# One kernel, one change: GpSimd copies the parts of the mixer's input with even and odd tokens side by side, and two attention groups load from the copies

## The chip, the cores and the metric

The kernel runs on one core of a Trainium2 chip. Its time is the device time of one execution in microseconds (us), as the median of several executions. The profile shows one further execution, instruction by instruction, for TensorE (PE, with its weight loads PEld), VectorE (DVE), ScalarE (ACT), GpSimd (POOL) and SyncE (SP, which issues DMAs).

## The reference, cut to what matters

The kernel computes two layers of a decoder trunk on 256 tokens of width 1024, all in float32. Each layer is a half-step of SwiGLU, a mixer, and another half-step of SwiGLU. The mixer normalises its input and multiplies it with one wide matrix; the columns feed three branches, of which the dilated attention is the one concerned:

```python
A_CONFIGS = ((128, 1), (512, 4), (2048, 16))      # (window, dilation) of the three head groups

def dilated_group(q, k, v, window, dilation):
    # gather each residue class mod dilation by stride, then banded attention inside each class
    ...

def hybrid_mixer(h, cos, sin, w_in, ...):
    a_qkv, b_q, b_kv, c_q, c_k, c_v, c_glow, c_r, gate_pre = jnp.split(h @ w_in, splits, axis=-1)
    a_q = apply_rope(rmsnorm(a_qkv[:, :, 0], a_q_norm), cos, sin)
    a_k = apply_rope(rmsnorm(a_qkv[:, :, 1], a_k_norm), cos, sin)
    y_a = dilated_mixer(a_q, a_k, a_qkv[:, :, 2])
    ...
    return merged @ w_out
```

## The kernel before, in words

**Precision and weights.** A float32 product is made of three fast passes (high x high, high x low, low x high), so every weight is split into a high part `hi` and a rest `lo`. `emit_dma` (L168) loads blocks of weights of up to 1 MB into a `raw` buffer. `emit_split` (L179) makes of each block one or two units: ACT casts `hi` (L191) and DVE subtracts to get `lo` (L192). A unit is 128 x 1024 numbers in nearly all cases. There are NRAW = 4 raw buffers and NHL = 5 pairs of `hi` and `lo`; `LD` and `LS` say how far ahead of their use the loads and splits are written. Every weight of the kernel goes through these buffers.

**The mixer's input.** `norm_parts` (L281) makes for each of the eight feature tiles one buffer `hl` of 128 features x 512: the high parts of the 256 tokens, then the low parts. The buffers named `a` in the profile come from one pool of NA.

**Projections.** `tok_proj` (L537) multiplies 512 columns of weights for two sets of 128 tokens. The tokens are what TensorE loads as its stationary 128 x 128 operand, the weights (512 columns) stream through it. For each feature tile k and each set there are three matmuls, L545 to L547. The two results lie in two PSUM banks `p`. The first head group takes tokens 0 to 127 and 128 to 255; the other two groups take the even tokens and the odd tokens (sets 2 and 3), and `tokens` (L306) reads them from `hl` with a step of two. Each of these two groups has three projections (q, k, v) in each of two layers, with 8 feature tiles x 2 sets x 3 = 48 matmuls each: 576 matmuls with a step of two in all.

**After a projection.** `rope` (L557) rotates the result. Of the mean square, DVE makes one number per token and head, and GpSimd raises it to the power -0.5 (`rsqrt`, L255, recorded as L256). For k, DVE takes that result (L601), multiplies the rotated rows with it (L603), and TensorE transposes them (`turned`, L583), before the scores can be computed.

**What sets the order.** The program is recorded by a tile framework whose scheduler fixes the order on each engine beforehand, from the data each instruction needs, the buffers that are free, and its own estimate of durations. On the chip each engine follows its list in order; an instruction whose data are not there holds up all behind it on that engine.

Of the kernel before, what the change touches and what calls it, by code (L numbers as in the profile page):

```python
# [11 lines left out]
F32R = mybir.dt.float32r  # L12
# [5 lines left out]
P = 128  # L18
T = 256
NT = T // P  # L20
# [51 lines left out]
def trunk_kernel(ctx, tc, x, positions, norm_ffn1, w_ffn1_in, w_ffn1_out, norm_mix, w_in, a_q_norm, a_k_norm,  # L72
                 b_q_norm, b_k_norm, b_sinks, c_gate_up, c_gate_bias, c_out_norm, w_branch, w_out,
                 norm_ffn2, w_ffn2_in, w_ffn2_out, const, out):
    nc = tc.nc
# [4 lines left out]
    sm = ctx.enter_context(tc.tile_pool(name="sm", bufs=1))  # L80
    pp = ctx.enter_context(tc.tile_pool(name="pp", bufs=1, space=PSUM))

    NA, NW, NRAW, NHL = 32, 12, 4, 5
    LD, LS = 4, 4
    uid = [0]

    def nm(s):
        uid[0] += 1
        return f"{s}{uid[0]}"

    def big(dt=F32):
        b = ap_.tile([P, 512], dt, tag="a", bufs=NA, name=nm("a"))
        return b
# [9 lines left out]
    def bank(tag):  # L103
        b = pp.tile([P, 512], F32, tag=tag, bufs=BANKS[tag], name=nm("p"))
        return b

    def f(a):
        return a.bitcast(F32)
# [21 lines left out]
    for l in range(DEPTH):  # L130
        for half in range(2):
# [8 lines left out]
            if l == DEPTH - 1 and half == 1:  # L140
                for e in range(2):
                    for k in range(0, KF, 4):
                        n = min(4, KF - k)
# [56 lines left out]
    def chunk():  # L200
        u = cur[0]
        cur[0] += 1
        ahead(u)
        return splits.pop(u)
# [69 lines left out]
    def begin_norm(which, l):  # L274
        n = Normed()
        n.col = which * 16 + l * 8
        n.hl, n.h, n.l = [], [], []
        n.acc, n.ssq = None, None
        return n

# [25 lines left out]
    def tokens(a, tt):  # L306

        return a[:, tt * P:(tt + 1) * P] if tt < NT else a[:, tt - NT:T:2]
# [46 lines left out]
    def joined(dst, ps):  # L355
        low = sm.tile([P, T], F32, tag="low", bufs=3, name=nm("low"))
        nc.scalar.copy(low, ps[:, T:2 * T])  # L357
        nc.vector.tensor_add(dst, ps[:, 0:T], low)  # L358

    n0 = begin_norm(0, 0)  # L360
    n0.src = []
    for mp in range(KD // 2):
# [153 lines left out]
    def mixer(l, n, nxt):  # L516
# [13 lines left out]
        def fill():  # L530
            for name in list(streams):
                owed[name] = owed.get(name, 0.0) + RATES[name]
                while owed[name] >= 1.0:
                    owed[name] -= 1.0
                    step(name)

        def tok_proj(cols, per, first=False, sets=(0, 1)):  # L537
            ps = [bank("mm") for _ in range(NT)]
            for k0 in range(0, KD, per):
                wh, wl = chunk()  # L540
                for k in range(k0, k0 + per):
                    for t in range(NT):
                        xh, xl = tokens(n.h[k], sets[t]), tokens(n.l[k], sets[t])
                        o = ps[t][:, 0:cols]
                        nc.tensor.matmul(o, xh, wh[:, k - k0, :], start=(k == 0), stop=False)  # L545
                        nc.tensor.matmul(o, xh, wl[:, k - k0, :], start=False, stop=False)  # L546
                        nc.tensor.matmul(o, xl, wh[:, k - k0, :], start=False, stop=(k == KD - 1))  # L547
                if not first:
                    fill()
            return ps  # L550
# [418 lines left out]


        psb = tok_proj(272, 4, True)
        next(fin)
        ps = bank("mm")
# [24 lines left out]
        for g in range(3):  # L998
            sets = (0, 1) if g == 0 else (2, 3)
            qs, sc = q_rope(tok_proj(512, 2, sets=sets), tabs[0], sets)  # L1000
            ks = k_rope(tok_proj(512, 2, sets=sets), tabs[1], 8, sets)
            v = v_side(tok_proj(512, 2, sets=sets), 0, 512, sets)
            ready.append(attend(qs, sc, ks, v, (C_MASK, C_MASK + 512, C_MASK + 640)[g], g == 0, lambda h: h // 2,
                                lambda h: h, None, group_stats(g), group_done(g)))
# [34 lines left out]
        for mp in range(KD // 2):  # L1039
# [13 lines left out]
            h, lo = big(F32R), big(F32R)  # L1053
# [15 lines left out]
    for l in range(DEPTH):  # L1069
        nmix = begin_norm(1, l)  # L1070
        swiglu(cur_n, lambda m: norm_tile(nmix, m), [lambda: late_loads(n0), lambda: None, late_gains, rope_tables] if l == 0 else (),
               first=keep_x if l == 0 else None)
        nf2 = begin_norm(2, l)
        mixer(l, nmix, lambda m: norm_tile(nf2, m))
        if l + 1 < DEPTH:
            cur_n = begin_norm(0, l + 1)
            swiglu(nf2, lambda m: norm_tile(cur_n, m))
        else:
            xo = [[None] * 2 for t in range(NT)]

            def token_major(t, e):
                def go():
                    ps = bank("at")
                    for i in range(4):
                        nc.tensor.transpose(ps[:, i * P:(i + 1) * P], xT[4 * e + i][:, t * P:(t + 1) * P], ident)
                    xo[t][e] = big()
                    nc.scalar.copy(xo[t][e], ps)
                return go

            swiglu(nf2, None, [lambda: None] * 2 + [token_major(t, e) for t in range(NT) for e in range(2)], True)  # L1090
# [25 lines left out]
```

## Time and profile before

| | |
|---|---|
| median of 3 runs | 1451.25 us (1451.22 to 1451.53) |
| profiled execution's own time | 1451.08 us |
| its span, first to last instruction | 1449.3 us |
| PE busy | 1436.9 us (99%) |
| DVE, ACT, POOL busy | 1047.5 us (72%), 840.5 us (58%), 135.1 us (9%) |
| mean share of the 16 DMA engines | 51.3% for the weights' queue |

The profile gives for each group of instructions their source line, the tiles they write and read (`p<-hi,a` writes a PSUM bank from a weight part and an input part), their number and mean duration, and what ended the idle time before them. Matmuls overlap: one of 512 columns is recorded with some 0.39 us, but the next starts earlier, so the cost of one is read from the distance of their starts. Some matmuls of plain float32 appear twice in the profile for one in the program.

### The profile page before, as it was taken

Reading aid. Unit: us, or ns where it says so; the run is one execution under the profiler, and the core shown is the slowest. Engines: PE = TensorE matmul, PEld = TensorE weight load, DVE = VectorE, ACT = ScalarE, POOL = GpSimd, SP = SyncE. Lnnn points to the kernel's source line nnn. Section 1 sums busy time; section 2 is a strip of 40 time slices with the busy share of each in tenths; the row PEclk is TensorE's granted clock in tenths of the full one; section 3 lists DMA queues with packets and bytes.
Section 4 is the critical chain, followed back from the end, with each engine's and each line's share of the span. In section 5 each row is a group of like instructions: output and inputs, shape, how many; then the busy total and the mean of one; then the engine's idle time right before and its main releaser. Section 6 shows DMA issues by size and latency. Waiting matters only on the chain.

```text
span 1449.3 us, 23359 instructions
## 1 busy us (share of the span) xinstructions
PE 1436.9 (99%) x9114; PEld 1268.9 (88%) x9114; DVE 1047.5 (72%) x1923; ACT 840.5 (58%) x1432; POOL 135.1 (9%) x124
## 2 busy tenths in 40 slices
PE   7999999999999999999999999999999999999998
PEld 6888898888899998888888888988878999988887
DVE  6787667888677686776677766688876767776753
ACT  6666456556747456665556655466477464566642
POOL 2030002223111000000000000032210200000000
PEclk9999999999999999999999999999999999999999
DMA  9655564443452565555556555643444426565551
GB/s 298 206 179 185 175 211 154 146 145 117 151 170 74 169 221 178 182 196 180 195 177 201 178 186 164 210 156 130 147 145 146 146 74 218 175 191 188 180 202 53
DMA packets 214702, 246.31 MB, mean 170 GB/s; under 512 B 6524, under 2 KB 183376, under 8 KB 214592
## 3 DMA queue, kind: packets, MB, share of 16 engines
q1 hardware_dynamic: 214016, 243.48, 51.3%
q0 software_dynamic: 544, 1.33, 0.4%
q8 instruction: 71, 1.16, 0.3%
q14 instruction: 39, 0.32, 0.1%
q10 hardware_dynamic: 32, 0.01, 0.0%
HBM read 243.76 MB, written 1.05 MB: 169 GB/s over the span
## 4 chain that ended last, share of the span: by engine, by line
PE 94%; DVE 2%; ACT 1%; POOL 1%; DMA 1%; issue 1%; SPq 0%; DVEq 0%
PE p L350 30%; PE p L353 16%; PE p L333 6%; PE p L331 6%; PE p L332 6%; PE p L545 6%; PE p L547 5%; PE p L546 5%; PE p L654 2%; PE p L690 2%; PE p L583 1%; PE p L491 1%; PE p L490 1%; PE p L492 1%; PE p L699 1%; PE p L878 1%
## 5 line engine op out<-in xcount | busy, mean ns | idle before, releaser
L191 ACT CAST hi<-raw 128x1024 fp32r<-128x1024 f32 (+3 forms) x468 | 483.1, 1036 | 475.8 <-PE p L350 234.1
L192 DVE TENSOR_TENSOR lo<-raw,hi 128x1024 fp32r<-128x1024 f32 (+3 forms) x468 | 561.6, 1206 | 241.6 <-PE p L353 141.1
L350 PE MATMUL p<-a,hi 128*128 128x512 f32 x1936 | 467.8, 393 | 2.9 <-ACT hi L191 1.5
L350 PEld LDWEIGHTS p<-a,hi 128*128 128x128 f32 x1936 | 355.5, 189 | 73.4 <-ACT hi L191 2.3
L353 PEld LDWEIGHTS p<-a,lo 128*128 128x128 f32 x1936 | 249.7, 191 | 10.3
L353 PE MATMUL p<-a,lo 128*128 128x256 f32 x1936 | 253.2, 283 | 0.0
L333 PE MATMUL p<-a,lo 128*128 128x256 f32 x768 | 219.1, 286 | 0.0
L331 PE MATMUL p<-a,hi 128*128 128x256 f32 x768 | 218.3, 286 | 0.0
L332 PE MATMUL p<-a,hi 128*128 128x256 f32 x768 | 218.1, 284 | 0.0
L256 POOL TENSOR_TENSOR s<-s,neghalf 128x8 f32<-128x8 f32 (+2 forms) x42 | 87.6, 2086 | 977.5 <-DVE s L316 656.9
L545 PE MATMUL p<-hi,a 128*128 128x512 f32 (+1 forms) x416 | 163.7, 394 | 0.0
L546 PE MATMUL p<-lo,a 128*128 128x512 f32 (+1 forms) x416 | 162.3, 390 | 0.0
L547 PE MATMUL p<-hi,a 128*128 128x512 f32 (+1 forms) x416 | 160.9, 389 | 0.0
L333 PEld LDWEIGHTS p<-a,lo 128*128 128x128 f32 x768 | 147.1, 192 | 1.4 <-issue 1.4
L332 PEld LDWEIGHTS p<-a,hi 128*128 128x128 f32 x768 | 147.2, 192 | 0.7 <-issue 0.3
L331 PEld LDWEIGHTS p<-a,hi 128*128 128x128 f32 x768 | 146.7, 192 | 1.1 <-issue 0.7
L545 PEld LDWEIGHTS p<-hi,a 128*128 128x128 f32 x416 | 79.3, 191 | 15.9 <-issue 0.7
L547 PEld LDWEIGHTS p<-hi,a 128*128 128x128 f32 x416 | 79.1, 191 | 15.0 <-issue 0.3
L546 PEld LDWEIGHTS p<-lo,a 128*128 128x128 f32 x416 | 79.4, 191 | 14.5 <-issue 0.3
L357 ACT COPY low<-p 128x256 f32<-128x256 f32 x200 | 73.7, 372 | 25.9 <-PE p L353 23.1
L358 DVE TENSOR_TENSOR w<-p,low 128x256 f32<-128x256 f32 x176 | 72.3, 416 | 0.0
L675 ACT ACTIVATE w<-w,st,s 128x128 f32<-128x128 f32 (+1 forms) x96 | 47.8, 503 | 11.7 <-DVE st L669 11.7
(224 smaller groups left out, 1290.5 us busy)
## 6 DMA issues: line engine op xcount, KB each, us to landing
raw<-in_w_ffn_in_dram SPq DMA_DIRECT2D x87, 1024.0 KB, 5.1
raw<-in_w_in_dram SPq DMA_DIRECT2D x76, 1024.0 KB, 5.0
raw<-in_w_ffn_out_dram SPq DMA_DIRECT2D x34, 1024.0 KB, 5.2
raw<-in_w_branch_dram SPq DMA_DIRECT2D x24, 512.0 KB, 3.4
raw<-in_w_ffn_out_dram SPq DMA_DIRECT2D x12, 768.0 KB, 4.5
raw<-in_w_out_dram SPq DMA_DIRECT2D x8, 1024.0 KB, 5.9
raw<-in_w_in_dram SPq DMA_DIRECT2D x4, 512.0 KB, 3.5
a<-in_x_dram SPq DMA_DIRECT2D x4, 256.0 KB, 5.1
```

The costliest lines, as they stand in the source:

```text
L191: nc.scalar.copy(hi[:, k:k + cut], r[:, k:k + cut])
L192: nc.vector.tensor_sub(lo[:, k:k + cut], r[:, k:k + cut], f(hi[:, k:k + cut]))
L256: nc.gpsimd.tensor_tensor(dst, src, neghalf[:, 0:n], op=OP.pow)
L331: nc.tensor.matmul(ps, wh, xh, start=first, stop=False)
L332: nc.tensor.matmul(ps, wh, xl, start=False, stop=False)
L333: nc.tensor.matmul(ps, wl, xh, start=False, stop=last)
L350: nc.tensor.matmul(ps, w[0][:, k, :], xhl[k], start=first and k == 0, stop=False)
L353: nc.tensor.matmul(ps[:, 0:T], w[1][:, k, :], xhl[k][:, 0:T], start=False, stop=last and k == nk - 1)
L357: nc.scalar.copy(low, ps[:, T:2 * T])
L545: nc.tensor.matmul(o, xh, wh[:, k - k0, :], start=(k == 0), stop=False)
L546: nc.tensor.matmul(o, xh, wl[:, k - k0, :], start=False, stop=False)
L547: nc.tensor.matmul(o, xl, wh[:, k - k0, :], start=False, stop=(k == KD - 1))
```

## The change

`tok_proj` no longer reads the even and odd tokens with a step. When the first projection with sets 2 and 3 comes to feature tile k, GpSimd copies `hl` of that tile into a new buffer `eo`, with the even tokens first and the odd ones behind them (both for the high and for the low parts), and all six projections of the layer's two groups load from the copies. That is 8 copies of 128 x 512 in a layer, 16 in all. To make room, the `a` pool grows by 8 buffers, and there is one raw buffer less and one pair of `hi` and `lo` less; loads and splits are written one step less ahead.

```diff
-    NA, NW, NRAW, NHL = 32, 12, 4, 5
-    LD, LS = 4, 4
+    NA, NW, NRAW, NHL = 40, 12, 3, 4
+    LD, LS = 3, 3
...
-        n.hl, n.h, n.l = [], [], []
+        n.hl, n.h, n.l, n.eo = [], [], [], []
...
-                        xh, xl = tokens(n.h[k], sets[t]), tokens(n.l[k], sets[t])
+                        if sets[t] < NT:
+                            xh, xl = tokens(n.h[k], sets[t]), tokens(n.l[k], sets[t])
+                        else:
+                            if len(n.eo) == k:
+                                n.eo.append(big(F32R))
+                                nc.gpsimd.tensor_copy(n.eo[k].rearrange("p (h o i) -> p h o i", h=2, o=2),
+                                                      f(n.hl[k]).rearrange("p (h i o) -> p h o i", h=2, o=2))
+                            xh, xl = (n.eo[k][:, h * T + (sets[t] - NT) * P:h * T + (sets[t] - NT + 1) * P] for h in range(2))
```

All later lines move down by seven: L545 to L547 become L552 to L554, L583 becomes L590, L603 becomes L610, L907 becomes L914.

The scheduler makes a new order of this. On TensorE in the first layer, where the first group's v projection (banks p310, p311) ends and the second group's q projection (p321, p322) begins, the order before is:

```order
L547 MATMUL p311_2623<-hi85_2572,a219_2098 128x512
L545 MATMUL p321_2716<-hi86_2626,a184_1650 128x512
...
L547 MATMUL p321_2716<-hi87_2653,a199_1806 128x512
L907 MATMUL p317_2703<-pair_88,w316_2651 128x2 x4
L583 MATMUL p323_2736<-cst_70,a277_2472 128x128 x4
L583 MATMUL p325_2743<-cst_70,a284_2488 128x128 x4
...
L546 MATMUL p321_2716<-lo88_2672,a205_1940 128x512
L583 MATMUL p327_2766<-cst_70,a297_2590 128x128 x4
L547 MATMUL p321_2716<-hi88_2671,a205_1940 128x512
```

Here a184 to a219 are the eight input parts `hl`, a277 and a284 the first group's rotated q, a297 its rotated k of tokens 0 to 127, and w316 a product for the gated linear attention. The same place with the change:

```order
L554 MATMUL p311_2617<-hi85_2618,a219_2092 128x512
L914 MATMUL p317_2697<-pair_88,w316_2643 128x2 x4
L590 MATMUL p325_2732<-cst_70,a277_2466 128x128 x4
L590 MATMUL p327_2739<-cst_70,a284_2482 128x128 x4
L590 MATMUL p331_2768<-cst_70,a297_2584 128x128 x4
L552 MATMUL p321_2710<-hi86_2647,a323_2716 128x512
...
L554 MATMUL p322_2711<-hi87_2663,a330_2760 128x512
L552 MATMUL p367_2922<-hi90_2748,a323_2716 128x512
```

The product of w316 and all three transposes, that of a297 among them, now stand ahead of the whole strided q projection, of which 26 matmuls stood before the transpose of a297 until now; behind its first four feature tiles (copies a323 to a330) comes the beginning of the next projection (p367).

On GpSimd at the same place, before; s301 and s308 are the powers for the first group's k of tokens 0 to 127 and 128 to 255:

```order
L256 TENSOR_TENSOR s288_2498<-s287_2496,neghalf_96 128x8
L256 TENSOR_TENSOR s301_2600<-s300_2598,neghalf_96 128x8
L256 TENSOR_TENSOR s308_2617<-s307_2615,neghalf_96 128x8
L256 TENSOR_TENSOR s350_2892<-s349_2890,neghalf_96 128x8
L256 TENSOR_TENSOR s357_2908<-s356_2906,neghalf_96 128x8
```

And with the change:

```order
L256 TENSOR_TENSOR s288_2492<-s287_2490,neghalf_96 128x8
L256 TENSOR_TENSOR s301_2594<-s300_2592,neghalf_96 128x8
L548 CAST a323_2716<-a184_1644 128x512
L548 CAST a324_2724<-a188_1655 128x512
L548 CAST a329_2752<-a195_1788 128x512
L548 CAST a330_2760<-a199_1800 128x512
L256 TENSOR_TENSOR s308_2611<-s307_2609,neghalf_96 128x8
L548 CAST a335_2786<-a205_1934 128x512
L548 CAST a336_2794<-a209_1946 128x512
L548 CAST a346_2857<-a215_2080 128x512
L548 CAST a347_2865<-a219_2092 128x512
```

All eight copies stand behind the power s301, four of them ahead of s308. In the second layer both engines show the same pattern.

## Rows read from the trace of the kernel before

**Rows 1.** The profile's page: busy us, share of the span, number of instructions.
```profile
PE 1436.9 (99%) x9114; PEld 1268.9 (88%) x9114; DVE 1047.5 (72%) x1923; ACT 840.5 (58%) x1432; POOL 135.1 (9%) x124
```

**Rows 2.** Waits of PE: line, releaser, us in total, times, longest.
```profile
PE p L260 <- DMA cst<-in_const_dram: 2.9, 1, 2.9
...
PE p L583 <- DVE a L603: 0.6, 2, 0.3
```

**Rows 3.** Two stretches of PE: length, PE busy (instructions), PEclk, DMA share, GB/s.
```profile
243.06:253.94 10.88, 10.88 (x50) 1.00 0.30 98
253.94:258.84 4.90, 4.90 (x22) 1.00 0.65 214
```

**Rows 4.** POOL's copies of 128 x 512: ns of one, min/median/max.
```profile
L765 POOL COPY w<-ce x8: 607/1102/1601, 419.1 to 1136.4; 128x512 f32<-128x512 f32 x8
```

**Rows 5.** PE in order of time, first layer: start, us, line, form, number.
```profile
253.94 0.39 PE L545 MATMUL p<-hi,a 128*128 128x512 f32 x1
...
258.84 0.95 PE L907 MATMUL p<-pair,w 128*128 128x2 f32 x8
259.65 1.07 PE L583 MATMUL p<-cst,a 128*128 128x128 f32 x8
260.47 0.48 PE L545 MATMUL p<-hi,a 128*128 128x512 f32 x1
...
262.20 0.65 PE L583 MATMUL p<-cst,a 128*128 128x128 f32 x4 [0.31 <-DVE a L603]
262.61 0.48 PE L547 MATMUL p<-hi,a 128*128 128x512 f32 x1
```

**Rows 6.** POOL in order of time: powers in both layers.
```profile
239.94 1.64 POOL L256 TENSOR_TENSOR s<-s,neghalf 128x8 f32<-128x8 f32 x1 [1.17 <-DVE s L575]
252.19 6.22 POOL L256 TENSOR_TENSOR s<-s,neghalf 128x8 f32<-128x8 f32 x1 [10.62 <-DVE s L575]
...
966.91 6.22 POOL L256 TENSOR_TENSOR s<-s,neghalf 128x8 f32<-128x8 f32 x1 [10.61 <-DVE s L575]
```

**Rows 7.** DVE in order of time around the first strided projection.
```profile
252.02 1.22 DVE L192 TENSOR_TENSOR lo<-raw,hi 128x1024 fp32r<-128x1024 f32 x1
...
255.56 0.68 DVE L901 TENSOR_TENSOR w<-a,a 128x512 f32<-128x512 f32 x1
...
256.50 0.42 DVE L893 TENSOR_TENSOR w<-a 128x256 f32<-128x256 f32 x1
258.45 0.23 DVE L601 TENSOR_SCALAR s<-s,s 128x8 f32<-128x8 f32 x1 [1.53 <-POOL s L256]
...
259.19 2.35 DVE L192 TENSOR_TENSOR lo<-raw,hi 128x1024 fp32r<-128x1024 f32 x2
261.45 0.69 DVE L603 TENSOR_TENSOR a<-a,s 128x512 f32<-128x512 f32 x1
```

**Rows 8.** DVE in order of time beside POOL's copies.
```profile
418.65 1.57 DVE L192 TENSOR_TENSOR lo<-raw,hi 128x1024 fp32r<-128x1024 f32 x1
```

**Rows 9.** PE in order of time, at the kernel's start and end.
```profile
8.74 0.80 PE L350 MATMUL p<-a,hi 128*128 128x512 f32 x1 [1.53 <-ACT hi L191]
...
10.89 2.69 PE L350 MATMUL p<-a,hi 128*128 128x512 f32 x5
...
13.92 3.90 PE L350 MATMUL p<-a,hi 128*128 128x512 f32 x14
...
1444.82 0.39 PE L492 MATMUL p<-hi,a 128*128 128x512 f32 x1
```

**Rows 10.** The last stretch: us, PE, PEld, DVE, ACT, POOL busy, PEclk.
```profile
1447.00:1449.00 2.00, 0.00 (x0) 0.00 (x0) 0.00 (x0) 0.00 (x0) 0.00 (x0) 0.58 0.21 70
```

**Rows 11.** ACT on the unit with the least reserve in the mixer.
```profile
245.97 1.06 ACT L191 CAST hi<-raw 128x1024 fp32r<-128x1024 f32 x1
```

**Rows 12.** PE's first use of that unit.
```profile
256.97 0.39 PE L546 MATMUL p<-lo,a 128*128 128x512 f32 x1
```

**Rows 13.** DMA issues of the mixer's weights: number, KB each, us to landing.
```profile
raw<-in_w_in_dram SPq DMA_DIRECT2D x76, 1024.0 KB, 5.0
```

## The prediction

> **What bounds the kernel now.** I read first the busy times of the engines: TensorE works in 1436.9 us of a span of 1449.3 us [rows 1], so the time is the sum of what stands on TensorE, plus its waits. Then its waits: the longest is 2.9 us at the kernel's start, and in the mixer there are only two of 0.3 us, both for the rotated k of the first head group [rows 2]. A gain can therefore come only from shorter matmuls, and any new wait of TensorE is lost in full, as nothing behind it has idle time in which to catch up. Third I read two adjoining stretches of TensorE's timeline, one that loads its tokens without a step and one with a step of two. Fourth I followed, on the timelines of TensorE, VectorE and GpSimd, what the new order makes TensorE wait for at the place where the strided work begins.
>
> **What the copies save.** From 243.06 to 253.94 TensorE starts 48 matmuls of 512 columns with adjacent tokens, in 10.88 us: 0.2267 us each. From 253.94 to 258.84 it starts 21 with every second token, in 4.90 us: 0.2333 us each [rows 3]. (The counts in the rows, 50 and 22, include matmuls that hang over from before.) The weights that stream through are the same in kind and the clock is 1.00 in both, so I put the 0.0067 us down to the step. The change takes it from 576 matmuls: 576 x 0.0067 = 3.8 us. If all of the difference had another source, the saving is zero.
>
> **What the copies cost on GpSimd.** Sixteen copies of 128 x 512. The nearest rows are GpSimd's copies of that size, 0.61 us at the least, 1.60 at the most [rows 4]; these read a broadcast operand and not every second number, so both ends stay bounds. I take 0.61, the undisturbed one. The copies themselves are off the path: TensorE spends six matmuls, 1.36 us, on each feature tile. The last four copies are wanted only after the first four tiles and the start of the next projection. If each took 1.6 us or more, that cover would be nearly gone; this is a rival below.
>
> **The wait that the new order adds.** This is the large term. Before, TensorE went at 253.94 straight into the strided q projection of the second group, because its operands had long been there [rows 5]. In the new order three things stand ahead of that projection: the product with w316 (L907, 0.81 us from its start to the next), eight transposes of q (L583, 0.82 us) and four transposes of a297 (0.41 us from 262.20 to 262.61) [rows 5]. TensorE takes its list in order, so the projection starts behind the last of them. And a297 is late, by this chain:
>
> - VectorE hands GpSimd the mean squares at about 252. The power that needs 1.64 us at 239.94 takes 6.22 us here, from 252.19 to 258.41 [rows 6]. VectorE works without a gap through subtractions, sums and products of two operands in SBUF until 256.92, and 1.5 us later the power is done [rows 7].
> - Then VectorE runs L601 at 258.45, a reduction, two subtractions of weights (L192), and only at 261.45 the product L603 that makes a297, which ends at 262.14 [rows 7]. TensorE begins the transposes at 262.20, after a wait of 0.31 us even in the kernel before [rows 5].
>
> None of these steps is earlier in the new order: each weight split there has the number one lower, but its buffer comes free with the same matmuls of TensorE. So the strided projection starts at 262.61 instead of 253.94, 8.67 us later. Of these, 0.81 + 0.82 + 0.41 = 2.04 us are work that is done earlier than before. The loss is 8.67 - 2.04 - 0.31 = 6.3 us. The second layer has the same order, and the same 6.22 us in the power at 966.91 [rows 6], so 6.3 us again.
>
> **What the copies add to this chain.** The first copies start at 258.41, behind the power, and meet VectorE's subtractions. A subtraction that started beside a copy took 1.57 us instead of 1.22 [rows 7, 8], about 0.4 us more. Two copies of 0.6 us fit ahead of the subtraction of 259.19, which then waits some 0.5 us for the second. What happens next has two bounds: either VectorE's subtractions follow each other so closely that no copy gets in, as the power of 252.19 did not (0.5 us in all), or copies and subtractions take turns and two more copies delay a297 by 0.6 us each (1.7 us). I take 0.5 us, by the row of the power. On this point the Trainium skill (SBUF — State Buffer, "Who interferes with whom") says that the engine that issues first holds the pair of ports for its whole instruction and the other is blocked until that one finishes. Read strictly, the power would have got in after the subtraction of 252.02; the row shows it waiting through all that follows until 256.92. By the strict reading the delay is 1.7 us, and the total 2.4 us more than by the row.
>
> **TensorE's clock.** In the new order TensorE stands idle from 253.94 until w316 is there (L901 ends at 256.24 [rows 7]), works 1.6 us and stands idle again until 262.2 or later. At the end of the kernel the last matmul starts at 1444.82 [rows 9], and in 1447 to 1449 the granted clock is 0.58 on average [rows 10]: it fell to the lower level (1.2 GHz, against 2.4 GHz at 1.00) within some 2 us of idleness. So I expect it to fall here too. What that costs is read at the start: work resumes at 8.74, five matmuls from 10.89 take 2.69 us, some 0.5 us each, and fourteen from 13.92 take 3.90 us, 0.28 us each [rows 9]. That is up to 5 us at half speed, a loss of at most 2.5 us; at the least nothing. I take 2.0 us in each layer, near the row, as part of those 5 us were waits. The Trainium skill (TensorE: Matmul & The Clock Gate, "Why this matters for your kernels") advises against idle gaps between bursts of matmuls for this reason; nothing in the sum hangs on it.
>
> **One weight buffer less of each kind.** A unit lasts 12 x 0.2267 = 2.7 us on TensorE, and with one pair fewer each cast may have to start that much later. The tightest unit in the mixer is cast at 245.97 [rows 11], its `lo` is done at 253.24 (the L192 of 252.02 [rows 7]), and TensorE reads it at 256.97 [rows 12]: 3.7 us of reserve, of which 1.0 us stays. A raw block lands in 5.0 us [rows 13], and three blocks of two units cover 16 us. So I cost these edits at nothing; if a unit like this one did come late, each layer would lose 1 to 2 us. At the start the later loads could move things by half a us either way.
>
> **The sum.** In each layer 6.3 + 0.5 + 2.0 = 8.8 us, twice 17.6 us, less 3.8 us: 13.8 us more. The profiled execution took 1451.1 us itself (span 1449.3 us and 1.8 us around it), within 0.2 us of the median of 1451.25. So 1451.1 + 13.8 = 1465 us.
>
> **Rivals.**
>
> - The stall without the fall of the clock: the 1.6 us of work between the two idle stretches may keep the clock up. Then 1465 - 4.0 = 1461 us. Against it stands the quick fall at the end of the kernel.
> - The copies rule: VectorE locks them out so that the first is done only after its run of products behind a297, some 3 us after that transpose, or each takes 1.6 us and more. Then each layer loses about 3 us more: 1471 us. For it speaks the power of 6.22 us; against it the free time between 258.41 and 259.19, in which one copy fits.
> - The buffers: units like the tightest come late in both layers, 1 to 2 us each: 1467 to 1469 us. Against it speaks the reserve that stays.
> - The other side: TensorE has no new wait. That needs a297 ready by about 256, so the power done in its 1.64 us and the subtractions behind the product. Only the 3.8 us would count: 1447.3 us. It decides once the product that makes a297 ends before TensorE has done the eight transposes of q. Against it: the power takes 6.22 us in both layers, and even a power of 1.64 us would leave L601 behind VectorE's list until 256.9, which takes back only 1.6 us a layer.
>
> **How the numbers follow.** Stall with the fall of the clock 0.55, without it 0.25, copies ruling 0.10, buffers 0.05, no stall 0.05. The range is 1459 to 1471 us: its lower end is 6.3 us a layer with neither port delay nor clock, 1460 us, with one us for the start; its upper end has the larger port delay (1.7), the larger clock loss (2.5) and, nearly, the copies' rival. A difference under 0.2% (2.9 us) counts as none, as that is about what a measurement of this kernel can tell. Slower 0.94; within 0.2% 0.02; faster 0.04, which is the last rival.
>
> **What the changed profile would show.** Right: strided groups gone, L552 to L554 at 0.227 us in all groups; two waits of PE on VectorE's L610 of 4 to 5 us, two on L908 of about 2 us; sixteen casts of L548 at 0.6 to 1.6 us on POOL behind a power of 6.2 us; PEclk under 1.00 in the stretch behind each stall; no new wait for L191. Wrong: PE's waits in the mixer stay under 1 us; or they stand at L552 and name POOL's cast (the copies rule) or ACT's cast (the buffers); or PEclk stays 1.00 (the first rival).

## The result and the profile after

The changed kernel takes 1489.76 us (median; 1488.68 to 1490.92) against 1451.28 us: ratio 1.0265, 95% interval 1.0253 to 1.0277, 38.5 us more. The prediction had the sign and the first place right (1465 us, 1459 to 1471) and the size wrong: 13.8 us were forecast, almost three times as much came. Lines behind the edit have moved by seven: L545 is now L552, L583 L590, L603 L610, L654 L661, L699 L706.

The page, which answers to [rows 1]:

```profile
PE 1452.1 (98%) x9114; PEld 1275.5 (86%) x9114; DVE 1049.1 (70%) x1923; ACT 840.6 (56%) x1432; POOL 146.7 (10%) x140
```

The same 9114 matmul records are busy for 15.2 us more than in [rows 1], although the strided loads are gone; the profiled span is 39.6 us longer, so some 24.4 us are new idleness. TensorE's waits (line, releaser, us in total, times, longest), which answer to [rows 2]:

```profile
PE p L590 <- DVE a L610: 10.2, 2, 5.1
PE p L552 <- DVE w L576: 6.4, 2, 3.2
PE p L914 <- DVE w L908: 4.6, 2, 2.3
...
PE p L552 <- ACT hi L191: 2.3, 2, 1.1
```

The first and the third are the stall that was forecast. The second was in no part of the prediction. The fourth stood only in its rival on the buffers (units cast late, 1 to 2 us a layer, chance 0.05), and its forecast said "no new wait for L191". In stretches of TensorE (length, PE busy, PEclk, DMA share, GB/s) the first two places of the first layer look like this:

```profile
254.00:258.00 4.00, 1.70 (x14) 1.00 0.40 111
258.00:262.00 4.00, 0.74 (x7) 0.71 0.43 166
262.00:266.00 4.00, 2.17 (x7) 0.50 0.52 163
266.00:270.00 4.00, 4.00 (x11) 0.51 0.26 99
270.00:274.00 4.00, 4.00 (x20) 1.00 0.00 0
360.00:364.00 4.00, 3.71 (x26) 1.00 0.00 1
364.00:368.00 4.00, 0.68 (x3) 0.69 0.06 6
368.00:372.00 4.00, 3.80 (x9) 0.50 0.75 260
```

The granted clock falls to 0.50 (1.2 GHz) twice in this layer, each time while TensorE stands idle, and stays there while work has resumed: from 266 to 270 it is busy throughout and does 11 matmuls, from 270 to 274 it does 20.

The first place in order of time: TensorE (answers to [rows 5]), GpSimd ([rows 6]), VectorE ([rows 7]).

```profile
256.79 1.02 PE L914 MATMUL p<-pair,w 128*128 128x2 f32 x8 [2.30 <-DVE w L908]
257.67 1.07 PE L590 MATMUL p<-cst,a 128*128 128x128 f32 x8
263.82 1.11 PE L590 MATMUL p<-cst,a 128*128 128x128 f32 x4 [5.08 <-DVE a L610]
264.59 0.77 PE L552 MATMUL p<-hi,a 128*128 128x512 f32 x1
```

```profile
252.58 6.23 POOL L256 TENSOR_TENSOR s<-s,neghalf 128x8 f32<-128x8 f32 x1 [10.62 <-DVE s L582]
258.76 4.46 POOL L548 CAST a<-a 128x512 fp32r<-128x512 f32 x4
```

```profile
258.84 0.59 DVE L608 TENSOR_SCALAR s<-s,s 128x8 f32<-128x8 f32 x1 [1.53 <-POOL s L256]
...
259.94 2.79 DVE L192 TENSOR_TENSOR lo<-raw,hi 128x1024 fp32r<-128x1024 f32 x2
262.65 1.12 DVE L610 TENSOR_TENSOR a<-a,s 128x512 f32<-128x512 f32 x1
```

This is the forecast chain, link by link: the power of 6.2 us, the copies behind it, the late L610, the transposes that wait. Beside the copies L608 takes 0.59 us and not 0.23, the two splits 2.79 and not 2.35, L610 1.12 and not 0.69 [rows 7]: 1.2 us, where the prediction took 0.5.

The second place, TensorE, ScalarE and VectorE of the changed kernel, then TensorE of the kernel before at the same work:

```profile
360.78 1.71 PE L661 MATMUL p<-a,a 64*128 64x128 f32 x16
362.42 2.56 PE L706 MATMUL p<-cst,w 128*128 128x128 f32 x8
368.20 0.76 PE L552 MATMUL p<-hi,a 128*128 128x512 f32 x1 [3.22 <-DVE w L576]
```

```profile
360.67 0.49 ACT L682 ACTIVATE w<-w,st,s 128x128 f32<-128x128 f32 x1 [3.67 <-DVE st L676]
...
364.50 1.03 ACT L191 CAST hi<-raw 128x1024 fp32r<-128x1024 f32 x1
365.44 0.59 ACT L569 ACTIVATE w<-p 128x512 f32<-128x512 f32 x1
```

```profile
365.56 1.23 DVE L192 TENSOR_TENSOR lo<-raw,hi 128x1024 fp32r<-128x1024 f32 x1 [1.62 <-ACT hi L191]
366.71 0.68 DVE L571 TENSOR_TENSOR a<-p,C 128x512 f32<-128x512 f32 x1
367.31 0.75 DVE L576 TENSOR_TENSOR w<-p,S 128x256 f32<-128x256 f32 x2
```

```profile
345.15 1.71 PE L654 MATMUL p<-a,a 64*128 64x128 f32 x16
346.79 0.51 PE L545 MATMUL p<-hi,a 128*128 128x512 f32 x1
347.14 0.27 PE L699 MATMUL p<-cst,w 128*128 128x128 f32 x1
347.17 0.49 PE L546 MATMUL p<-lo,a 128*128 128x512 f32 x1
347.49 0.39 PE L547 MATMUL p<-hi,a 128*128 128x512 f32 x1
347.72 0.27 PE L699 MATMUL p<-cst,w 128*128 128x128 f32 x1
```

Before, the transposes of eight exponentials (L699) stood one by one among strided matmuls, so TensorE worked while ScalarE made the next exponential. In the new list eight score matmuls (L661; each stands twice in the profile, as x16 in all) and then the eight transposes (L706) stand in a block: TensorE goes at the pace of the exponentials, and only behind the eighth does ScalarE come to the cast of 364.50. VectorE waits 1.62 us for this cast with its split (L192). Behind the split, in VectorE's list, stand the rope's products (L571, L576), which empty the bank that the next projection needs; they end at 368.06, and TensorE resumes at 368.20.

### The profile page after: what moved, and what is told of

Same layout as the page of the kernel before. It is cut to its first block, busy times and chain, and to the rows that moved or that the text cites. A ratio compares the mean times of both kernels' runs of the same rounds, so it can differ in the third digit from the quotient of the medians.

```text
span 1488.9 us, 23347 instructions
## 1 busy us (share of the span) xinstructions
PE 1452.1 (98%) x9114; PEld 1275.5 (86%) x9114; DVE 1049.1 (70%) x1923; ACT 840.6 (56%) x1432; POOL 146.7 (10%) x140
## 3 DMA queue, kind: packets, MB, share of 16 engines
q8 instruction: 71, 1.16, 0.3%
## 4 chain that ended last, share of the span: by engine, by line
PE 91%; DVE 3%; issue 2%; ACT 2%; POOL 1%; DMA 1%; SPq 0%; DVEq 0%; POOLq 0%
PE p L350 29%; PE p L353 15%; PE p L331 6%; PE p L333 6%; PE p L332 6%; PE p L552 5%; PE p L554 5%; PE p L553 5%; PE p L661 2%; PE p L697 2%; PE p L590 2%; PE p L492 1%; PE p L490 1%; PE p L491 1%; PE p L885 1%
## 5 line engine op out<-in xcount | busy, mean ns | idle before, releaser
L192 DVE TENSOR_TENSOR lo<-raw,hi 128x1024 fp32r<-128x1024 f32 (+3 forms) x468 | 562.0, 1209 | 285.6 <-ACT hi L191 121.1
L191 ACT CAST hi<-raw 128x1024 fp32r<-128x1024 f32 (+3 forms) x468 | 483.3, 1037 | 487.5 <-PE p L350 222.0
L552 PE MATMUL p<-hi,a 128*128 128x512 f32 (+1 forms) x416 | 165.5, 402 | 8.7 <-DVE w L576 6.4
L554 PE MATMUL p<-hi,a 128*128 128x512 f32 (+1 forms) x416 | 163.1, 394 | 0.0
L552 PEld LDWEIGHTS p<-hi,a 128*128 128x128 f32 x416 | 80.3, 193 | 26.7 <-issue 7.4
L554 PEld LDWEIGHTS p<-hi,a 128*128 128x128 f32 x416 | 79.8, 192 | 17.2 <-issue 0.7
```

Source lines behind the costliest of these rows:

```text
L191: nc.scalar.copy(hi[:, k:k + cut], r[:, k:k + cut])
L192: nc.vector.tensor_sub(lo[:, k:k + cut], r[:, k:k + cut], f(hi[:, k:k + cut]))
```

## Where each layer's time goes

TensorE's two lists have many points at which both have done the same matmuls. Subtracting the two traces there (changed kernel less e1_buffers_alone, below) gives for the first layer:

| place (us in the changed kernel) | us lost |
|---|---|
| 254 to 290, strided projection begins late, clock low; from 275 on a block of score matmuls is split in four (1.2) | 11.4 |
| 291 to 294, score matmuls no longer in pairs | 1.3 |
| 363 to 374, transposes in a block, clock low | 6.5 |
| 409 to 411.5, two waits for ScalarE's cast | 1.9 |
| small differences elsewhere (321 to 420) | -1.6 |

The second layer loses 10.7, 1.3, 6.1 and 1.9 us at the same places. Only the late beginning and the low clock of the first row were forecast.

## The experiments

Every kernel here was timed beside the kernel before, in five rounds; the ratio's 95% interval stands in brackets.

**e1_buffers_alone**, all but the copies:

```diff
-    NA, NW, NRAW, NHL = 32, 12, 4, 5
-    LD, LS = 4, 4
+    NA, NW, NRAW, NHL = 40, 12, 3, 4
+    LD, LS = 3, 3
```

> The change without its copies: 40 buffers of the kind a, one raw block and one pair of split weights less, one load and one split less ahead; the strided loads stay. TensorE's list is that of before at the two places where the changed kernel stands idle; a few rows move elsewhere. My theory (the order that the copies bring costs the time; the buffers cost nothing): 1451 us, within 0.2% of before, no wait of TensorE over 1 us in the mixer, the granted clock at 1.00 throughout. Rival (fewer split weights let casts and rope come late, which made the later waits at L552): 1455 to 1470 us, with waits of TensorE for L191.

Measured: 1452.85 us, 1.0011 [1.0002, 1.0020]. No wait over 1 us in the mixer, clock 1.00. So the buffers cost about 1.7 us (the kernel before took 1451.16 us beside it) and not nothing; 1.0 us in each layer goes at one place (445 us), where this list, too, parts score matmuls that ran in pairs. Before, 24 records stood together, sixteen of them in eight pairs, and took 2.05 us; here they are parted into eight (1.16 us, none in a pair) and sixteen (1.71 us).

**e2_copies_alone**, the reverse: the copies, with the four numbers of before.

> The change with the weight buffers and the 32 buffers a of before: only the copies and the loads from them. TensorE's list has the product with w316, eight transposes of q and four of a297 ahead of the strided projection, as in the changed kernel. My theory (the copies' order costs the time): two waits of 2.3 and 5 us in each layer at the same place, the clock falls behind them, 1480 to 1492 us. Rival (the buffers make the later waits at L552, 4.4 us a layer and the second fall of the clock): only the first place stays, 1465 to 1475 us.

Measured: 1494.88 us, 1.0301 [1.0287, 1.0315], a little above the first theory's range. The first place stands as in the changed kernel; later the list differs again and brings waits of its own. Its waits of TensorE:

```profile
PE p L590 <- DVE a L610: 9.7, 2, 5.1
PE p L661 <- ACT a L626: 7.4, 2, 3.7
PE p L914 <- DVE w L908: 4.6, 2, 2.3
```

The fewer buffers are not needed for a loss of this size, and the rival's number falls. The later waits stand mostly at other lines than in the changed kernel (L661): each list has its own later places.

**e3_copies_vector_early**, copies ahead of the loop over head groups, by VectorE:

```diff
+        for k in range(KD):
+            n.eo.append(big(F32R))
+            nc.vector.tensor_copy(n.eo[k].rearrange("p (h o i) -> p h o i", h=2, o=2),
+                                  f(n.hl[k]).rearrange("p (h i o) -> p h o i", h=2, o=2))
         for g in range(3):
```

> The buffers of the change; the sixteen copies stand ahead of the first head group's projections and are made by VectorE. TensorE's and ScalarE's lists are those of e1_buffers_alone, row for row; VectorE's list is that list with the copies put in. My theory (order, not loads or buffers): no idle stretch at the start of the strided projection; e1's time less up to 3.8 us (576 matmuls x 0.0067 us), so 1447 to 1450 us; VectorE's copies, 0.5 us each, may make one product of rope late by 1 to 2 us. Rival (reading from the copies is what slows TensorE): as slow as the changed kernel, over 1480 us.

Measured: 1450.57 us, 0.9996 [0.9987, 1.0005], just above the range (1447 to 1450 us). Loading from the copies costs nothing; the rival falls. Thirty-six matmuls in a row, first strided (e1), then from the copies (e3):

```profile
299.07:307.47 8.40, 8.40 (x38) 1.00 0.38 125
```

```profile
298.76:306.92 8.16, 8.16 (x37) 1.00 0.39 129
```

8.40/36 is 0.2333 us and 8.16/36 is 0.2267: the step costs 0.0067 us here, as in [rows 3].

**e4_copies_gpsimd_early**, the same loop with `nc.gpsimd.tensor_copy`, right behind the first feature product.

> The buffers of the change; the sixteen copies stay on GpSimd but are written behind the first feature product, so they stand on GpSimd ahead of the power of the norm. TensorE's list is nearly that of e1_buffers_alone (84 rows of 8288 moved). My theory: no idle stretch at the strided projection; the norm's power comes some 5 us later (8 x 0.64 us), which TensorE may wait for by up to 2 us a layer; 1447 to 1455 us. Rival (GpSimd's copies beside VectorE's two-operand products are what delays the chain): VectorE and TensorE lose 5 us a layer wherever the copies stand, 1460 us or more.

Measured: 1457.87 us, 1.0047 [1.0035, 1.0060]: between the two theories, and 5.0 us slower than e1. My reason for a loss was wrong: the norm's power came no later (211.48 against 211.56 us in e1), since GpSimd made the copies as soon as each part was there. But VectorE's list differs from e1's: weight splits stand ahead of the rope of the narrow k, whose product L572 ends at 222 us, and TensorE waits for it:

```profile
222.25 0.77 PE L548 MATMUL p<-hi,a 128*128 128x512 f32 x1 [2.60 <-DVE w L572]
```

**e5_order_alone**: no copies, but TensorE's list written out. `listed` holds every matmul and transpose in the order of the code, `ORDER` the list to be had, here that of the changed kernel:

```diff
+    rank = [i for a, n in ORDER for i in range(a, a + n)]
+    for a, b in zip(rank[:-1], rank[1:]):
+        tc.add_manual_dep(listed[b].ins, listed[a].ins.name,
+                          mybir.DependencyInfo(mybir.DependencyClass.NoSync, mybir.DependencyReason.DATA),
+                          reason="order")
```

> No copies, strided loads as before, the buffers of e1_buffers_alone; only TensorE's list is written out to be that of the changed kernel, row for row (ScalarE's list comes out the same as there, VectorE's but for two rows). Theory 1 (the order costs the time, the copies nothing but their own saving): the changed kernel's 1489.8 us plus the 3.8 us that strided loads cost, less up to 1 us of port delay: 1491 to 1494 us, with the waits at L907, L583 and L545 and the falls of the clock as there. Theory 2 (the copies themselves, by delaying VectorE and by coming late, make half of it): 1465 to 1475 us.

Measured: 1489.92 us, 1.0265 [1.0251, 1.0279]: the changed kernel's time without a single copy, and 1.1 us below the first theory's range. The order is the loss. That means the order as a whole: with TensorE's list the planner gave VectorE and ScalarE the changed kernel's lists too, but for a few rows, and no run parts the three. Its wait for a297 is shorter than the changed kernel's 5.08 us by the 1.24 us that the copies add:

```profile
262.30 1.11 PE L584 MATMUL p<-cst,a 128*128 128x128 f32 x4 [3.84 <-DVE a L604]
```

Against it the changed kernel gains about 2.1 us at L552 to L554 and loses 2 x 1.24 us here: the copies come out even.

**e6_order_first_place**: e1's list, with the changed kernel's in the 119 matmuls at the first place only.

> As e5, but TensorE's list is that of e1_buffers_alone except for the stretch where the strided projection of the second group begins (119 matmuls in each layer), which is in the changed kernel's order. Theory 1 (each place costs by itself): 1452.9 us + 2 x (2.3 + 5.1 us of waits - 0.3 + 3.0 us of the first low clock, 10.2 us of which TensorE works 6.1) = 1473 us. Rival (the later waits, 4.4 us a layer, and the second fall of the clock only follow from the lateness that the first place brings): 1483 us or more.

Measured: 1472.58 us, 1.0148 [1.0134, 1.0161]. The number is the first theory's, but in part by luck. Its term of 5.1 us was the wait with the copies; without them TensorE waits 3.8 and 3.0 us for a297:

```profile
PE p L584 <- DVE a L604: 6.8, 2, 3.8
```

What is missing there is made up in the main by the score matmuls that this stretch splits into smaller groups, 1.3 us a layer, which the theory had left out.

**e7_order_rest**: the complement, all places but the first.

> As e5, but with the stretch at the beginning of the strided projection in the order of e1_buffers_alone, the rest of the mixer in the changed kernel's. Theory 1 (each place costs by itself): 1452.9 us + 2 x (3.2 + 1.1 us of waits + 2.0 us of the second low clock + some 2 us of matmuls of half height that no longer run in pairs) = 1468 to 1471 us, waits at L545 only. Rival (they follow from the first place): 1455 to 1460 us.

Measured: 1470.68 us, 1.0132 [1.0118, 1.0146], with the waits at the later places unchanged (3.2 and 1.1 us a layer). Both totals are as the first theory had them, and they add up: 19.7 us (e6 less e1) and 17.8 us (e7 less e1) on 1452.85 make 1490.4, against 1489.92 in e5. The later places do not follow from the first.

**e8_gpsimd_early_order_kept**: e3's loop with GpSimd's copies, and e1's list written out as in e5.

> The buffers of the change; the sixteen copies on GpSimd, written ahead of the first head group, so behind the norm's powers and ahead of the first power of rope; TensorE's list written out to be that of e1_buffers_alone. Theory 1 (place and order, not the engine): the copies, 8 x 0.62 = 5 us, are done before the strided projection needs them; the first power of rope may come up to 5 us later, which moves the rotated q of the first group, wanted at 247 us, 0 to 3 us a layer; 1449 to 1456 us. Rival (copies on GpSimd beside VectorE cost by the port wherever they stand): 1460 us or more.

Measured: 1451.01 us, 0.9998 [0.9989, 1.0007], inside the first theory's range. GpSimd is no worse a place for the copies than VectorE, as long as TensorE's list stays.

**e9_after_idle_filled**: the changed kernel, its list written out, with twenty unused matmuls in the first idle stretch.

```diff
+            if fill:
+                filled[len(listed)] = [nc.tensor.matmul(ps, n.h[0][:, 0:P], n.hl[0], start=True, stop=True)
+                                       for _ in range(fill)]
```

> The changed kernel with its lists as they are; in each layer TensorE does 20 more matmuls of 512 columns (into the bank that the late transposes of a297 overwrite right after), 20 x 0.227 = 4.5 us, in the 5.1 us in which it stands idle for a297. They do no work that is used. Theory 1 (idleness brings the clock down, and that costs 3.0 us in the 6.1 us of work behind the first stall): the granted clock stays at 1.00 there, the rest of the wait stays, and the time falls by 6 us to 1484 us. Rival (the clock falls for another reason, such as the 2.3 us of idleness ahead of it): no gain, 1489 to 1491 us.

Measured: 1487.01 us, 1.0249 [1.0235, 1.0263]: 2.8 us less, the profiled run 4.4 us less; 6 were expected. The intervals overlap, but all four executions (1486.06 to 1488.49) lie below the changed kernel's (1488.68 to 1490.92). The trace shows why it is less. First layer, three stretches from the filling on:

```profile
258.00:262.00 4.00, 4.00 (x22) 1.00 0.36 140
262.00:266.00 4.00, 3.39 (x17) 1.00 0.45 125
266.00:270.00 4.00, 4.00 (x19) 1.00 0.35 137
```

The clock stays at 1.00, and of the forecast 3.0 us 2.8 are won. In the second layer it had fallen at 989.5 (the mean of 0.69 from 988 to 992 is 1.00 up to there and 0.50 behind it), after the 2.3 us wait and two short bursts, just as the filling began:

```profile
988.00:992.00 4.00, 4.00 (x21) 0.69 0.67 245
```

```profile
989.75 6.33 PE L592 MATMUL p<-a 128*128 128x512 f32 x20
```

There the twenty ran in part at half speed and took 6.3 us, not 4.5, and made the transposes late; 1.6 us were won. So in the first layer the 5.1 us of idleness bring the clock down, and the fill shows the price of that fall (2.8 us) but not that of both; the rival's 2.3 us gap is enough in one layer of two.

**e10_order_later_place**: as e6, for the 55 matmuls ahead of the second stall.

> As e6_order_first_place, but only the stretch ahead of the second stall (55 matmuls in each layer) stands in the changed kernel's order: the second sixteen score matmuls directly ahead of the transposes of their exponentials, without the strided matmuls between. No copies. Theory 1 (this place makes the waits at L545 for the rope's product by itself): 1452.9 us + 2 x 6.5 us (0.7 + 0.4 us of transposes paced by ScalarE, 3.5 us of wait, 1.9 us of low clock) = 1466 us. Rival (the stall needs the lateness of the places before it): under 1457 us.

Measured: 1466.69 us, 1.0110 [1.0094, 1.0125], as forecast: 6.9 us a layer from this place alone, with the same wait:

```profile
355.51 0.76 PE L546 MATMUL p<-hi,a 128*128 128x512 f32 x1 [3.22 <-DVE w L570]
```

**e11_copies_vector_more_pairs**: e3 with five pairs of split weights.

```diff
-    NA, NW, NRAW, NHL = 40, 12, 3, 4
-    LD, LS = 3, 3
+    NA, NW, NRAW, NHL = 36, 12, 3, 5
+    LD, LS = 3, 4
```

> As e3_copies_vector_early with 36 buffers of the kind a, three raw blocks, but five pairs of split weights as in the kernel before; TensorE's list is nearly that of before. My theory: the 2.3 us that the copies save remain, and the 1.4 us that e1 lost by fewer buffers come back in part: 1448 to 1450.5 us. Rival (what e1 lost is due to the raw blocks, which stay at three): 1450.5 us, as e3.

Measured: 1450.01 us, 0.9991 [0.9982, 1.0000]. It is the fastest of all, 1.2 us under the kernel before, which the measurement just fails to tell from none. It lies in the first theory's range, but is too near the rival's 1450.5 us to decide between them.

**e12_copies_unused**: the changed kernel's copies are made, TensorE goes on with strided loads.

```diff
-                            xh, xl = (n.eo[k][:, h * T + (sets[t] - NT) * P:h * T + (sets[t] - NT + 1) * P] for h in range(2))
+                            xh, xl = tokens(n.h[k], sets[t]), tokens(n.l[k], sets[t])
```

> The changed kernel, with the copies made by GpSimd where it makes them (all eight of a layer behind the four powers of the first head group), but TensorE goes on loading every second token from the uncopied parts, so nobody waits for a copy. Its list is then that of e1_buffers_alone, row for row, as is VectorE's. Theory 1 (the order costs, the copies on GpSimd cost little): 1452.9 us as e1, up to 1 us a layer more where a copy meets VectorE's products, so 1452.5 to 1455 us. Theory 2 (the copies themselves slow VectorE, and through it TensorE): 1460 us or more.

Measured: 1453.07 us, 1.0013 [1.0004, 1.0022], as e1. TensorE's list is e1's again, so it is the dependence of the strided matmuls on the copies that changes it, not the copies. Copies that nobody waits for cost nothing, though they meet VectorE's work (1.03 us each on average, against 0.64 us undisturbed). They stand later here, at 265.5 and not at 258.76, so what they cost at the changed kernel's place is shown by e5 alone:

```profile
265.52 8.27 POOL L548 CAST a<-a 128x512 fp32r<-128x512 f32 x8
```

## Why the prediction was right in kind and wrong in size

- **What bounds the kernel**: right. Every new wait of TensorE was lost in full.
- **The step that failed** is the sum itself, "in each layer 6.3 + 0.5 + 2.0": it has one place. The new list was followed where the strided work begins and taken to cost nothing everywhere behind it, without a reason. Behind it lie 17.8 us (e7), most of the 24.7 us by which the forecast fell short; of these 13.8 us are the blocked transposes (e10), the rest is the two waits for casts and the score matmuls out of their pairs, less small gains. I had looked for waits where the diff touches the code; the list moves wherever the attention stream is interleaved with those matmuls.
- **The first place**: right in its chain, with one term missing. Idle 2.30 + 5.08 - 0.31 = 7.1 us a layer against 6.3 + 0.5. Without copies the wait is 1.24 us shorter (e5), so the stall is 5.8 us and was taken slightly too large, and the port term is 1.2 us and was taken too small, between its bounds of 0.5 and 1.7 us. The rule of the Trainium skill (SBUF — State Buffer, "Who interferes with whom"), read strictly, fits the copies, which took turns with the splits (4.46 us for four, not 4 x 0.64), and not the power, which again waited 6.23 us through VectorE's run of products. The sum had no term for the block of score matmuls that is split behind this stall (1.2 us a layer).
- **The clock**: the fall was right, its size 3.0 instead of 2.0 us at the first place (TensorE works from 263.8 to 269.9 at 0.50, half of 6.1 us; e9 won back 2.8). A second fall, 365.5 to 372.3 us, came with the second place.
- **What the copies save**: 2.3 us (the medians of e3 and e1), not 3.8. The 0.0067 us hold where strided matmuls follow each other; over all 576 the mean is 0.004 (2.3/576), as less is won where transposes and scores stand between them.
- **The copies' own time**: 0.64 us each at the median, and no wait of TensorE names them; right.
- **Buffers at nothing**: 1.7 us, through the list and not through late weights: e1 has no wait for a cast in the mixer. The sign "no new wait for L191" was wrong: the changed kernel waits 1.1 us a layer. These waits are in e7 as well and not in e1, so they come with the list; whether that list would wait here, or at the second place, with all the buffers of before, no run shows.
- **The rivals**: the one without a fall of the clock and the copies rule were wrong. The buffers' rival had a loss of the right size (1.9 us a layer at 409 us), but by itself it accounts for a tenth of the time lost. The other side, no new wait, is what e3, e8 and e11 show: with the list kept, 1450.0 to 1451.0 us. The 1447.3 us of that rival would also have needed the full 3.8 us and the free buffers.

## What to carry to other kernels

Where a planner sets the order, a new operand in front of a few matmuls can move hundreds of others (here 543 places of the list in each layer, e5 against e8): compare the two lists over the whole stretch in which the streams are interleaved, and cost each place where they differ, not only the place of the edit. To separate an edit from the order that it brings, keep the edit and drop its dependence (e12), or impose the new order on the old code (e5). Make such helper copies early enough that nothing is planned around them, and look at the lists even then: e4 made them early and lost 5.0 us against e1, with a changed order.

## What the hardware showed

**Score matmuls in pairs.** The matmuls of half height (64 rows) take about half the time if neighbours in the list use different halves of the rows. (In this kernel the two halves also write different banks; no run parts the two.) Eight matmuls, two records each, in the kernel before, in which the halves alternate; then the same eight in the changed kernel, one half at a time:

```profile
279.60 1.17 PE L878 MATMUL p<-w 64*128 64x128 f32 x16
```

```profile
291.25 1.16 PE L885 MATMUL p<-w 64*128 64x128 f32 x8
...
293.00 1.16 PE L885 MATMUL p<-w 64*128 64x128 f32 x8
```

Eight records take as long as sixteen did. The Trainium skill (TensorE: Matmul & The Clock Gate, "Part 3: Packing small matmuls — row/col tiling") says that matmuls on different groups of rows run at the same time; the trace agrees, and shows that the order of the list decides whether they do.

**A short gap can be enough for the clock.** In e9's second layer it fell to 1.2 GHz after an idle stretch of 2.3 us and two short bursts, in the first layer it did not after the same work.

**VectorE copies faster.** The copy of 128 x 512 with a step took VectorE 0.42 us (e3) and GpSimd 0.64 us undisturbed.
